# Three heads folded on GpSimd, four heads biased on GpSimd in the middle stages, and the last ScalarE sums moved to the end of a streamed log-sum-exp

## The chip, the cores and the metric

The kernel runs on one core of a Trainium2 chip. The metric is the device time of one execution in microseconds (us). In the profile PE is TensorE, DVE is VectorE, ACT is ScalarE, POOL is GpSimd and SP issues the loads. All runs with more than one execution were of the fast state; for a run of one execution (a "look", with its profile) the state is unknown. Positions such as "318.5" are us from the start of the span of one profiled execution.

## The reference

```python
def setup_inputs():                      # cut
    B, S, D, H = 8, 2048, 2048, 8
    x    = randn(B, S, D)                # float32, 134 MB
    bias = randn(H, D // H)

def reference(x, bias):
    x_heads = x.reshape(B, S, H, 256).transpose(0, 2, 1, 3) + bias[None, :, None, :]
    x_tiled = np.repeat(x_heads, 2, axis=2)
    mx = x_tiled.max(axis=-1, keepdims=True)
    return mx.squeeze(-1) + np.log(np.exp(x_tiled - mx).sum(axis=-1))
```

For each row and each head of 256 columns the result is the log of a sum of exponentials, written twice. The kernel works without the maximum. Since exp(x + b) = exp(x) exp(b), a head can get its bias before the exponential (an addition) or after it (a product with the "weight" exp(b)).

## The kernel before

A unit is two rows on each of 128 partitions, 2 MB, and there are 64 of them (0 to 63), in nine buffers. Late units are worked in halves: 62.1 is the second half of unit 62. The heads of a row are shared out in three ways:

- heads below `pe`: TensorE adds the bias into PSUM, ScalarE takes the exponential and its sum;
- heads from `g0` on: GpSimd adds the bias, ScalarE takes the exponential, VectorE sums (`later`);
- heads between: ScalarE takes the exponential at once, VectorE multiplies by the weights and sums in one instruction (`weigh`). With `late=True` (most of the run) their exponential is taken together with that of the GpSimd heads, and VectorE multiplies and sums in two instructions. Weights of heads 1 to 4 lie in PSUM (`w_ps`), those of heads 5 to 7 in SBUF (`w_sb`).

```python
BULK   = dict(pe=2, g0=4, late=True)
MIXED  = dict(pe=1, g0=5, late=False)
PROMPT = dict(pe=2, g0=8, late=False)
STAGES = [(0, BULK, False), (49, MIXED, False), (57, MIXED, True), (61, PROMPT, True)]
LAST_CUTS = [[0, 512, 1280, 2048], [0, 512, 1536, 2048]]
# ... cut ...
    def g_add(m, t, k0, k1):                       # GpSimd
        c = m["g0"] * Dh
        v = xts[t % NBUF][:, k0:k1, c:D]
        add = nc.gpsimd.tensor_tensor(
            out=v, in0=v, in1=each_row(b_rep, c - G0, D - c, k1 - k0), op=ALU.add
        )
        return on_x(t, add, [loads[t, k0, 0]])
# ... cut ...
    def weigh(t, v, h, dst, after):                # VectorE, one head
        c = h * Dh
        w = w_ps[:, c - W0 : c - W0 + Dh] if c < W1 else w_sb[:, c - W1 : c - W1 + Dh]
        ttr = nc.vector.tensor_tensor_reduce(out=v, in0=v, in1=w, # ... cut ...
                                             accum_out=dst)
# ... cut: the main loop, for each piece of columns ...
            if h0 < h1 and not m["late"]:
                done = exp_inplace(t, xt[:, k0:k1, h0 * Dh : h1 * Dh], loads[t, k0, c0])
            if for_pe and (c0 == 0 or c1 == D):
                for_pe()                           # ScalarE sums of the half before
                for_pe = None
            if not m["late"]:
                for k in range(k0, k1):
                    for h in range(h0, h1):
                        weigh(t, xt[:, k, h * Dh : (h + 1) * Dh], h, sums[:, k, h : h + 1], done)
```

Of the kernel before, what the change touches and what calls it, by code (L numbers as in the profile page):

```python
# [12 lines left out]
ALU = mybir.AluOpType  # L13


K = 2
NBUF = 9
# [2 lines left out]



BULK = dict(pe=2, g0=4, late=True)
MIXED = dict(pe=1, g0=5, late=False)
PROMPT = dict(pe=2, g0=8, late=False)

STAGES = [(0, BULK, False), (49, MIXED, False), (57, MIXED, True), (61, PROMPT, True)]

LAST_CUTS = [[0, 512, 1280, 2048], [0, 512, 1536, 2048]]


@with_exitstack
def kernel(
# [6 lines left out]
    nc = tc.nc  # L40
    P = nc.NUM_PARTITIONS
    B, S, D = x.shape
    H, Dh = bias.shape
    assert D == H * Dh and S % (P * K) == 0
    NBLK = S // (P * K)
    T = B * NBLK
# [3 lines left out]
    W0, G0, W1 = Dh, 4 * Dh, 5 * Dh  # L50
# [8 lines left out]
    w_sb = sb.tile([P, D - W1], F32, name="w_sb")  # L59
# [11 lines left out]
    xts = [sb.tile([P, K, D], F32, name=f"xt{i}") for i in range(NBUF)]  # L71
# [2 lines left out]
    tpair = pp.tile([P, 2, K, P], F32, name="tpair")  # L74
    tps = [tpair[:, i] for i in range(2)]

    def mode_of(t):
        return [m for t0, m, _ in STAGES if t0 <= t][-1]

    def halves_of(t):  # L80
        return [s for t0, _, s in STAGES if t0 <= t][-1]

    def pieces(t):

        if not halves_of(t):
            return [(0, K, 0, D)]
        cuts = [[0, D]] * K if t < T - 1 else LAST_CUTS
        return [
            (k, k + 1, c0, c1) for k in range(K) for c0, c1 in zip(cuts[k], cuts[k][1:])
        ]  # L90

    def rows_of(t):

# [10 lines left out]
    def on_x(t, ins, after):  # L104
        known = [u for u in users[t] if u.ins.engine != ins.ins.engine]
        for before in range(t % NBUF, t, NBUF):
            known += users[before]
        for u in known:
            if u not in after:
                tc.declare_no_dep(  # L110
                    ins.ins, u.ins, reason="waited for by those it waits for"
                )
        users[t].append(ins)
        return ins
# [53 lines left out]
    for i, c in enumerate(range(G0, D, MM)):  # L168
        spread(ps[i], c, c + MM)
        nc.scalar.activation(  # L170
            out=b_rep[:, c - G0 : c - G0 + MM], in_=ps[i], func=ACT.Copy
# [10 lines left out]
    def add_bias(m, t, k0, k1):  # L182


        n = m["pe"] * Dh
        xt = xts[t % NBUF]
        step = MM // n
        groups = [(k, min(k + step, k1)) for k in range(k0, k1, step)]
        got = []
        for ka, kb in groups:  # L190
            p = ps[n_ps[0] % len(ps)]
            n_ps[0] += 1
            nc.tensor.matmul(  # L193
                p[:, 0 : (kb - ka) * n],
                lhsT=ones3,
                rhs=each_row(b3, 0, n, kb - ka),
                start=True,
                stop=False,
            )
            got.append([p[:, k * n : (k + 1) * n] for k in range(kb - ka)])  # L200
        rows = []
        for (ka, kb), views in zip(groups, got):
            p = views[0]
            mm = nc.tensor.matmul(  # L204
                bass.AP(
                    tensor=p.tensor,
                    offset=p.offset,
                    ap=[p.ap[0], [1, (kb - ka) * n]],
                ),
                lhsT=ident,  # L210
                rhs=xt[:, ka:kb, 0:n],
                start=False,
                stop=True,
            )
            on_x(t, mm, [loads[t, k0, 0]])
            rows += [(v, mm) for v in views]
        return rows
# [21 lines left out]
    def g_add(m, t, k0, k1):  # L239
# [7 lines that stand above are left out]
    def exp_inplace(t, v, after):  # L247
        return on_x(t, nc.scalar.activation(out=v, in_=v, func=ACT.Exp), [after])  # L248

    def later(m, t, k0, k1, sums, add):  # L250

        h0 = m["pe"] if m["late"] else m["g0"]
        v = xts[t % NBUF][:, k0:k1, h0 * Dh : D]
        done = exp_inplace(t, v, add)
        if m["late"]:
            n = (m["g0"] - h0) * Dh
            f = v[:, :, 0:n]
            mul = nc.vector.tensor_tensor(  # L258
                out=f,
                in0=f,  # L260
                in1=each_row(w_ps, h0 * Dh - W0, n, k1 - k0),
                op=ALU.mult,
            )
            done = on_x(t, mul, [done])
        red = nc.vector.tensor_reduce(  # L265
            out=sums[:, k0:k1, h0:H],
            in_=v.rearrange("p k (h j) -> p k h j", j=Dh),
            op=ALU.add,
            axis=mybir.AxisListType.X,
        )  # L270
        last_uses[t].append(on_x(t, red, [done]))

    def weigh(t, v, h, dst, after):
        c = h * Dh
        w = w_ps[:, c - W0 : c - W0 + Dh] if c < W1 else w_sb[:, c - W1 : c - W1 + Dh]
        ttr = nc.vector.tensor_tensor_reduce(  # L276
            out=v,
            in0=v,
            in1=w,
            scale=1.0,  # L280
            scalar=0.0,
            op0=ALU.mult,
            op1=ALU.add,
            accum_out=dst,
        )
        last_uses[t].append(on_x(t, ttr, [after]))

    def finish(b):

        nr = H * NBLK  # L290
        tp = tps[b % 2]
        for k in range(K):
            nc.tensor.transpose(  # L293
                out=tp[0:nr, k],
                in_=R[b][:, k].rearrange("p h n -> p (h n)"),
                identity=ident,
            )
        tv = bass.AP(
            tensor=tp.tensor,
            offset=tp.offset,  # L300
            ap=[[tp.ap[0][0], nr], [1, P], [P, K], [0, 2]],
        )
        nc.scalar.activation(out=res[:, b], in_=tv, func=ACT.Ln)  # L303

    def store():

        nc.sync.dma_start(
            out=out[0 : B - 1].rearrange("b h (n r) -> (h n) b r", n=NBLK),
            in_=res.rearrange("q b p k r -> q b (p k r)"),
        )  # L310
# [16 lines left out]
    def sums_of(t):  # L327

        b, blk = divmod(t, NBLK)
        if b < B - 1:  # L330
            return R[b][:, :, :, blk]
        return R_last[:, :, blk, :].rearrange("p h k -> p k h")


    for_pool = for_pe = None
    for t in range(T):
        m = mode_of(t)
        xt = xts[t % NBUF]
        sums = sums_of(t)
        for k0, k1, c0, c1 in pieces(t):  # L340
            add = None
            if c0 == 0:
                got = add_bias(m, t, k0, k1)
                if m["g0"] < H:
                    add = g_add(m, t, k0, k1)
            if for_pool:
                for_pool()
                for_pool = None
            h0 = max(c0 // Dh, m["pe"])
            h1 = min(c1 // Dh, m["g0"])  # L350
            if h0 < h1 and not m["late"]:
                done = exp_inplace(
                    t, xt[:, k0:k1, h0 * Dh : h1 * Dh], loads[t, k0, c0]
                )
            if for_pe and (c0 == 0 or c1 == D):
                for_pe()
                for_pe = None
            if not m["late"]:
                for k in range(k0, k1):
                    for h in range(h0, h1):  # L360
                        weigh(
                            t,
                            xt[:, k, h * Dh : (h + 1) * Dh],
                            h,
                            sums[:, k, h : h + 1],
                            done,
                        )

            def pool_part(t=t, m=m, k0=k0, k1=k1, sums=sums, add=add):
                if add:  # L370
                    later(m, t, k0, k1, sums, add)
                if k1 == K and t + NBUF < T:
                    load(t + NBUF)

            def pe_part(t=t, m=m, got=got, k0=k0, k1=k1, sums=sums):
                for k in range(k0, k1):
                    sum_biased(m, t, k, *got[k - k0], sums)

            for_pool = pool_part
            if c0 == 0:  # L380
                if m["g0"] < H:
                    pe_part()
                else:
                    for_pe = pe_part

        fb, at = divmod(t - 2, NBLK)
        if fb >= 0 and at == NBLK - 1:
            finish(fb)
            if fb == B - 2:
                store()  # L390
    for_pe and for_pe()
    finish_last()

    order.__exit__(None, None, None)
# [30 lines left out]
```

## Time and profile before

| | before |
|---|---|
| time, median of 3 | 328.97 us (328.75 to 329.11) |
| span of the profiled execution | 327.38 us |
| last load lands | 320.10 us |
| half 62.1 lands | 315.00 us |
| VectorE's last instruction ends | 323.58 us |

The prediction shows the lines behind this table. A convenient clock for the end is the landing of 62.1, the last large load: VectorE ended 323.58 - 315.00 = 8.58 us after it. This number is "the tail" below.

### The profile page before, as it was taken

How to read it: one execution, taken by the hardware profiler on the slowest of the kernel's cores; microseconds unless marked ns; L12 is line 12 of the kernel's file. 1: busy time of each engine (PE TensorE's matmuls, PEld its weight loads, DVE VectorE, ACT ScalarE, POOL GpSimd, SP SyncE). 2: the span in 40 equal slices, each digit the busy share in tenths (PEclk: the TensorE clock that was granted, in tenths of full speed). 3: DMA queues.
4: the chain of work that ended last, by engine and by line, in shares of the span. 5: the costliest groups of instructions: out<-in, count | busy, mean ns of one | idle time of the engine just before them, and what ended most of it. 6: DMA issues, size and time to landing. Idle time of an engine off the chain costs nothing.

```text
span 327.4 us, 1988 instructions
## 1 busy us (share of the span) xinstructions
PE 227.0 (69%) x383; PEld 66.3 (20%) x383; DVE 288.4 (88%) x380; ACT 278.1 (85%) x567; POOL 270.8 (83%) x79
## 2 busy tenths in 40 slices
PE   5496766757767769967676967795756446476792
PEld 2131221211211212221121212221211101122220
DVE  0019999999999999999999899989998999999994
ACT  3279999699899888989888889889888988899894
POOL 6999899989999999999998999999989667697400
PEclk9999877797698775777967597659778555555557
DMA  7999999999999999999999999999999999999991
GB/s 293 431 428 434 427 426 428 428 424 432 426 426 431 426 430 425 426 432 425 424 433 424 423 432 426 430 430 424 428 429 422 434 428 416 422 418 423 420 394 52
DMA packets 11647, 135.41 MB, mean 414 GB/s; under 512 B 1330, under 2 KB 1458, under 8 KB 2674
## 3 DMA queue, kind: packets, MB, share of 16 engines
q1 hardware_dynamic: 11536, 135.27, 97.8%
q8 instruction: 3, 0.05, 0.1%
q14 instruction: 10, 0.07, 0.1%
q10 hardware_dynamic: 2, 0.01, 0.0%
q0 software_dynamic: 96, 0.00, 0.0%
HBM read 134.23 MB, written 1.05 MB: 413 GB/s over the span
## 4 chain that ended last, share of the span: by engine, by line
DMA 57%; DVE 24%; PE 6%; POOL 6%; ACT 5%; issue 1%; SPq 0%; DVEq 0%
DMA xt<-in_x_dram 54%; DVE R L265 17%; DVE xt L258 6%; PE ps L204 5%; ACT xt L248 4%; POOL xt L242 4%; DMA b<-bparts 2%; PE ps L193 1%; ACT xt L223 1%; DMA brow<-in_bias_dram 1%; DVE xt L276 1%; POOL brest L157 0%; POOL brest L155 0%; POOL b L160 0%; POOL bparts L156 0%
## 5 line engine op out<-in xcount | busy, mean ns | idle before, releaser
L242 POOL TENSOR_TENSOR xt<-xt,b_rep 128x2048 f32<-128x2048 f32 (+2 forms) x65 | 264.5, 4071 | 33.1 <-DMA xt<-in_x_dram 33.0
L204 PE MATMUL ps<-xt,ident 128*128 128x512 f32 (+1 forms) x240 | 175.2, 863 | 80.9 <-DMA xt<-in_x_dram 80.6
L248 ACT ACTIVATE xt<-xt 128x3072 f32<-128x3072 f32 (+3 forms) x89 | 186.3, 2114 | 18.5 <-POOL xt L242 16.3
L265 DVE TENSOR_REDUCE R<-xt 128x12 f32<-128x3072 f32 (+1 forms) x56 | 176.6, 3154 | 1.7
L223 ACT ACTIVATE xt<-ps 128x256 f32<-128x256 f32 x232 | 86.7, 398 | 15.6 <-PE ps L204 15.1
L258 DVE TENSOR_TENSOR xt<-xt,w_ps 128x1024 f32<-128x1024 f32 x49 | 59.7, 1218 | 32.4 <-ACT xt L248 32.2
L204 PEld LDWEIGHTS ps<-xt,ident 128*128 128x128 f32 x240 | 54.4, 256 | 157.3 <-DMA xt<-in_x_dram 117.5
L223 ACT ACTIVATION_READ_ACCUMULATOR xt<-ps 128x1 f32 x232 | 51.3, 223 | 0.0
L193 PE MATMUL ps<-b,ones 3*128 3x512 bf16 (+1 forms) x120 | 46.5, 454 | 5.6 <-DMA b<-bparts 3.5
L276 DVE CUSTOM_DVE_ANT_0 xt<-xt,w_ps 128x256 f32<-128x256 f32 x114 | 40.6, 418 | 0.3 <-ACT xt L248 0.3
L193 PEld LDWEIGHTS <-ones 3*128 3x128 bf16 x120 | 7.7, 96 | 78.1 <-issue 78.1
L265 DVE TENSOR_REDUCE R_last<-xt 128x3 f32<-128x768 f32 (+1 forms) x9 | 9.4, 1042 | 0.0
L276 DVE CUSTOM_DVE_ANT_0 xt<-xt,w_sb 128x256 f32<-128x256 f32 x18 | 6.7, 426 | 0.0
L276 DVE DVE_READ_ACCUMULATOR2_ANT R_last<- 128x1 f32 x76 | 6.6, 87 | 0.0
L164 PE MATMUL ps<-brow,ones 1*128 1x512 f32 x4 | 3.7, 1089 | 3.4 <-DMA brow<-in_bias_dram 3.4
L293 PE MATMUL tpair<-ident,R 128*64 128x128 f32 x14 | 3.5, 340 | 3.8 <-DVE R L265 3.8
L303 ACT ACTIVATE res<-tpair 64x512 f32<-64x512 f32 x7 | 4.1, 584 | 2.3 <-PE tpair L293 2.3
L170 ACT ACTIVATE b_rep<-ps 128x512 f32<-128x512 f32 x2 | 1.2, 597 | 4.6 <-PE ps L164 4.6
L276 DVE DVE_READ_ACCUMULATOR2_ANT R<- 128x1 f32 x56 | 4.7, 84 | 0.0
L164 PE MATMUL w_ps<-brow,ones 1*128 1x512 f32 x4 | 4.0, 1096 | 0.7 <-ACT w_ps L176 0.7
L176 ACT ACTIVATE w_ps<-w_ps 128x512 f32<-128x512 f32 x2 | 1.2, 582 | 3.3 <-PE w_ps L164 3.3
L293 PEld LDWEIGHTS tpair<-ident,R 128*64 128x64 f32 x14 | 1.6, 139 | 10.9 <-DVE R L265 8.0
(21 smaller groups left out, 12.4 us busy)
## 6 DMA issues: line engine op xcount, KB each, us to landing
xt<-in_x_dram SPq DMA_DIRECT2D x57, 2048.0 KB, 32.0
xt<-in_x_dram SPq DMA_DIRECT2D x12, 1024.0 KB, 24.7
out_dram<-res SPq DMA_DIRECT2D x1, 896.0 KB, 9.8
xt<-in_x_dram SPq DMA_DIRECT2D x3, 256.0 KB, 14.1
xt<-in_x_dram SPq DMA_DIRECT2D x2, 384.0 KB, 15.8
xt<-in_x_dram SPq DMA_DIRECT2D x1, 512.0 KB, 12.0
out_dram<-res_last SPq DMA_DIRECT2D x1, 128.0 KB, 1.7
b<-bparts POOLq DMA_DIRECT2D x3, 1.0 KB, 5.5
```

Of the source, the lines that this page charges most:

```text
L164: nc.tensor.matmul(dst, lhsT=ones, rhs=brow[:, c0:c1], start=True, stop=True)
L170: nc.scalar.activation(out=b_rep[:, c - G0 : c - G0 + MM], in_=ps[i], func=ACT.Copy)
L193: nc.tensor.matmul(p[:, 0 : (kb - ka) * n], lhsT=ones3, rhs=each_row(b3, 0, n, kb - ka), start=True, stop=False,)
L204: mm = nc.tensor.matmul(bass.AP(tensor=p.tensor, offset=p.offset, ap=[p.ap[0], [1, (kb - ka) * n]],), lhsT=ident, rhs=xt[:, ka:kb, 0:n], s ...
L223: act = nc.scalar.activation(out=xts[t % NBUF][:, k, c : c + Dh], in_=p[:, c : c + Dh], func=ACT.Exp, accum_out=sums[:, k, h : h + 1],)
L242: add = nc.gpsimd.tensor_tensor(out=v, in0=v, in1=each_row(b_rep, c - G0, D - c, k1 - k0), op=ALU.add)
L248: return on_x(t, nc.scalar.activation(out=v, in_=v, func=ACT.Exp), [after])
L258: mul = nc.vector.tensor_tensor(out=f, in0=f, in1=each_row(w_ps, h0 * Dh - W0, n, k1 - k0), op=ALU.mult,)
L265: red = nc.vector.tensor_reduce(out=sums[:, k0:k1, h0:H], in_=v.rearrange("p k (h j) -> p k h j", j=Dh), op=ALU.add, axis=mybir.AxisListTy ...
L276: ttr = nc.vector.tensor_tensor_reduce(out=v, in0=v, in1=w, scale=1.0, scalar=0.0, op0=ALU.mult, op1=ALU.add, accum_out=dst,)
L293: nc.tensor.transpose(out=tp[0:nr, k], in_=R[b][:, k].rearrange("p h n -> p (h n)"), identity=ident,)
L303: nc.scalar.activation(out=res[:, b], in_=tv, func=ACT.Ln)
```

## The change

Its intent is to take work off VectorE, which has hardly a pause in the last 70 us: (a) four heads in place of three with GpSimd bias in the middle stages, and the stages' starts moved; (b) GpSimd multiplies three heads of the last units (one of 62.1, two of 63.0) by their weights and folds them from 256 to 32 columns, so that VectorE is left with a small reduce; (c) new cuts of the last unit, and its ScalarE sums at the very end.

```diff
-MIXED = dict(pe=1, g0=5, late=False)
+MIXED = dict(pe=1, g0=4, late=False, fold=0)
+PROMPT_F1 = dict(pe=2, g0=8, late=False, fold=1)
+PROMPT_F2 = dict(pe=2, g0=8, late=False, fold=2)
+FOLD = 32
+STAGES = [(0, (BULK,)), (50, (MIXED,)), (56, (MIXED, MIXED)), (61, (PROMPT, PROMPT)),
+          (62, (PROMPT, PROMPT_F1)), (63, (PROMPT_F2, PROMPT))]
+LAST_COLS = [[(0, 512), (1280, 2048), (512, 1280)],
+             [(0, 512), (512, 1024), (1024, 1536), (1536, 2048)]]
 ... (cut) ...
+    def fold(t, k, h0, h1, sums, after):
+        v = xts[t % NBUF][:, k, h0 * Dh : h1 * Dh]
+        done = nc.gpsimd.tensor_tensor(
+            out=v, in0=v, in1=w_sb[:, h0 * Dh - W1 : h1 * Dh - W1], op=ALU.mult
+        )
+        ... (cut: while n > FOLD, GpSimd adds the upper half of each head to the lower) ...
+        def add_up():
+            red = nc.vector.tensor_reduce(out=sums[:, k, h0:h1], in_=v[:, :, 0:FOLD], ...)
+        return add_up
 ... (cut) ...
-            if for_pool:
-                for_pool()
+            if c0 == 0 and (t < T - 1 or k0 == 0):
+                flush(for_pool)
 ... (cut) ...
+                if hf < h1:
+                    for_pool.append(fold(t, k0, hf, h1, sums, done))
-            if for_pe and (c0 == 0 or c1 == D):
-                for_pe()
+            if c0 == 0 and (t < T - 1 or k0 == 0):
+                flush(for_pe)
```

The lists are STAGES and LAST_COLS with fewer line breaks than in the file.

More of the change, by code (lines that the diff above doesn't have):

```diff
@@ L17 @@
 NBUF = 9
-BULK = dict(pe=2, g0=4, late=True)
-MIXED = dict(pe=1, g0=5, late=False)
-PROMPT = dict(pe=2, g0=8, late=False)
-STAGES = [(0, BULK, False), (49, MIXED, False), (57, MIXED, True), (61, PROMPT, True)]
-LAST_CUTS = [[0, 512, 1280, 2048], [0, 512, 1536, 2048]]
+BULK = dict(pe=2, g0=4, late=True, fold=0)
+MIXED = dict(pe=1, g0=4, late=False, fold=0)
+PROMPT = dict(pe=2, g0=8, late=False, fold=0)
+PROMPT_F1 = dict(pe=2, g0=8, late=False, fold=1)
+PROMPT_F2 = dict(pe=2, g0=8, late=False, fold=2)
+FOLD = 32
+STAGES = [
+    (0, (BULK,)),
+    (50, (MIXED,)),
+    (56, (MIXED, MIXED)),
+    (61, (PROMPT, PROMPT)),
+    (62, (PROMPT, PROMPT_F1)),
+    (63, (PROMPT_F2, PROMPT)),
+]
+LAST_COLS = [
+    [(0, 512), (1280, 2048), (512, 1280)],
+    [(0, 512), (512, 1024), (1024, 1536), (1536, 2048)],
+]
 @with_exitstack
@@ L75, with modes_of @@
     tps = [tpair[:, i] for i in range(2)]
-    def mode_of(t):
-        return [m for t0, m, _ in STAGES if t0 <= t][-1]
-    def halves_of(t):
-        return [s for t0, _, s in STAGES if t0 <= t][-1]
+    def modes_of(t):
+        return [modes for t0, modes in STAGES if t0 <= t][-1]
     def pieces(t):
-        if not halves_of(t):
+        if len(modes_of(t)) == 1:
             return [(0, K, 0, D)]
-        cuts = [[0, D]] * K if t < T - 1 else LAST_CUTS
-        return [
-            (k, k + 1, c0, c1) for k in range(K) for c0, c1 in zip(cuts[k], cuts[k][1:])
-        ]
+        cols = [[(0, D)]] * K if t < T - 1 else LAST_COLS
+        return [(k, k + 1, c0, c1) for k in range(K) for c0, c1 in cols[k]]
     def rows_of(t):
@@ L286, in weigh @@
         last_uses[t].append(on_x(t, ttr, [after]))
+    def fold(t, k, h0, h1, sums, after):
[3 more added lines that the diff above has]
+        )
+        on_x(t, done, [after])
+        v = v.rearrange("p (h j) -> p h j", j=Dh)
+        n = Dh
+        while n > FOLD:
+            n //= 2
+            done = nc.gpsimd.tensor_tensor(
+                out=v[:, :, 0:n], in0=v[:, :, 0:n], in1=v[:, :, n : 2 * n], op=ALU.add
+            )
+            on_x(t, done, [])
+        def add_up():
+            red = nc.vector.tensor_reduce(
+                out=sums[:, k, h0:h1],
+                in_=v[:, :, 0:FOLD],
+                op=ALU.add,
+                axis=mybir.AxisListType.X,
+            )
+            on_x(t, red, [done])
+        return add_up
     def finish(b):
@@ L332, in sums_of, with flush @@
         return R_last[:, :, blk, :].rearrange("p h k -> p k h")
-    for_pool = for_pe = None
+    for_pool = []
+    for_pe = []
+    def flush(later_work):
+        for f in later_work:
+            f()
+        later_work.clear()
     for t in range(T):
-        m = mode_of(t)
         xt = xts[t % NBUF]
@@ L340 @@
         for k0, k1, c0, c1 in pieces(t):
+            m = modes_of(t)[k0]
             add = None
@@ L345 @@
                     add = g_add(m, t, k0, k1)
-            if for_pool:
-                for_pool()
-                for_pool = None
+            if c0 == 0 and (t < T - 1 or k0 == 0):
+                flush(for_pool)
             h0 = max(c0 // Dh, m["pe"])
             h1 = min(c1 // Dh, m["g0"])
+            hf = max(h0, min(h1, H - m["fold"]))
             if h0 < h1 and not m["late"]:
@@ L354 @@
                 )
-            if for_pe and (c0 == 0 or c1 == D):
-                for_pe()
-                for_pe = None
+                if hf < h1:
+                    for_pool.append(fold(t, k0, hf, h1, sums, done))
+            if c0 == 0 and (t < T - 1 or k0 == 0):
+                flush(for_pe)
             if not m["late"]:
                 for k in range(k0, k1):
-                    for h in range(h0, h1):
+                    for h in range(h0, hf):
                         weigh(
@@ L377, in pe_part @@
                     sum_biased(m, t, k, *got[k - k0], sums)
-            for_pool = pool_part
+            for_pool.append(pool_part)
             if c0 == 0:
@@ L383 @@
                 else:
-                    for_pe = pe_part
+                    for_pe.append(pe_part)
         fb, at = divmod(t - 2, NBLK)
@@ L390 @@
                 store()
-    for_pe and for_pe()
+    flush(for_pe)
+    flush(for_pool)
     finish_last()
```

## The prediction

> **What bounds the kernel now.** I read the page first (busy digits, DMA row, chain of waits), then the chain in order of time for the last 20 us, then the timeline of the end. A unit is two rows of 2048 numbers on each of 128 partitions (2 MB); there are 64, numbered 0 to 63, and the late ones are worked in two halves (62.0, 62.1). A head is 256 columns.
>
> ```profile
> PE 227.0 (69%) x383; PEld 66.3 (20%) x383; DVE 288.4 (88%) x380; ACT 278.1 (85%) x567; POOL 270.8 (83%) x79
> ...
> DMA  7999999999999999999999999999999999999991
> GB/s 293 431 428 434 427 426 428 428 424 432 426 426 431 426 430 425 426 432 425 424 433 424 423 432 426 430 430 424 428 429 422 434 428 416 422 418 423 420 394 52
> ...
> DMA 57%; DVE 24%; PE 6%; POOL 6%; ACT 5%; issue 1%; SPq 0%; DVEq 0%
> ```
>
> The DMA row is 9 in all but its first and last slice: 134 MB come in at about 425 GB/s without a hole. That stream ends at about 320.1 us of a 327.4 us span, and no part of the change makes it shorter. So only what follows the last landing can be won. When does it end? The loads' own view gives the last issue at 309.9 us and the shortest issue-to-landing time, which is that of the last small piece: 309.94 + 10.16 = 320.10.
>
> ```profile
> L125 SPq DMA_DIRECT2D xt<-in_x_dram x5: 327/327/328, 300.0 to 309.9; - x5
> ...
> DMA to landing us min/median/max: 10.2/13.5/16.6
> ```
>
> What follows it is in the chain by time and the timeline:
>
> ```profile
> 319.62 0.84 ACT xt L223 x4
> 320.46 0.95 ACT xt L248
> 321.41 0.03 issue
> 321.44 0.42 DVE xt L276
> ...
> 323.58 0.02 DVE R_last L276
> 323.60 0.14 issue
> 323.73 0.46 PE tpair L314
> 324.19 0.02 issue
> 324.22 0.38 ACT res_last L320
> ```
>
> Two ScalarE sums (L223) stand ahead of the exponential of the last row (L248), and VectorE waits for that and then works six heads (L276, one every 0.342 us) until 323.58. Transpose, Ln and store take 327.38 - 323.58 = 3.80 us and are untouched. VectorE itself has no idle time from 253.2 us to its end but 0.34 us at 321.4: it lags from the middle stages on, so its work there counts too.
>
> **What the Trainium skill says.** "GPSIMD Engine Reference", section 3.1, has an fp32 GpSimd tensor_tensor of 2048 columns at 4497 ns; this trace agrees (4540). "VectorE: DVE Perf Modes", section "The perf-mode tier table", leaves fp32 tensor_tensor and tensor_reduce at one element a cycle; the trace agrees (1024 columns of product took 1218 ns, 3072 of reduce 3354 ns). "SBUF — State Buffer", section "Who interferes with whom", says that a VectorE instruction with two SBUF inputs contends with a GpSimd one that reads SBUF, and that the second to issue "fully blocks". Before, nothing shows it: the L276 rows that read w_sb (two SBUF inputs) start at 311.7, and GpSimd's last instruction ends at 306.8. After, they overlap.
>
> **The change part by part.** Durations come from these rows of the groups kept apart by shape:
>
> ```profile
> L242 POOL TENSOR_TENSOR xt<-xt,b_rep 128x2048 f32<-128x2048 f32 x49 | 222.4, 4540 | 18.7 <-DMA xt<-in_x_dram 18.7
> ...
> L242 POOL TENSOR_TENSOR xt<-xt,b_rep 128x768 f32<-128x768 f32 x8 | 14.5, 1819 | 3.8 <-DMA xt<-in_x_dram 3.8
> L265 DVE TENSOR_REDUCE R_last<-xt 128x3 f32<-128x768 f32 x8 | 7.6, 953 | 0.0
> L276 DVE CUSTOM_DVE_ANT_0 xt<-xt,w_sb 128x256 f32<-128x256 f32 x18 | 6.7, 426 | 0.0
> ```
>
> A straight line through the GpSimd rows is 0.18 us + 2.13 ns a column; through the reduces (953 ns for 768, 1751 for 1536) 0.15 us + 1.04 ns. What I read off these lines is an estimate.
>
> (a) Middle stages, four biased heads on GpSimd. Per half VectorE loses one head (0.34) and its reduce grows by 256 columns (0.27): 2.22 becomes 2.15 us. ScalarE's two exponentials swap sizes (1024 + 768 columns), sum equal. GpSimd goes from 1.82 to 2.36 us per half, while a half lands every 2.48 us. Unit 49 goes back to the bulk form (VectorE 4.6 us in place of 4.4, starting later). If only VectorE counted, eleven such units (22 halves) would win 22 x 0.07 = 1.5 us, less 0.5 for unit 49: about 1.1. But GpSimd enters the halves 2.1 us late (unit 55: 280.1 + 4.6 = 284.7, while 56.0 has landed at 282.6), and catches up only 2.48 - 2.32 = 0.16 a half. It ends 60.1 near 307.95, against 306.83 before. The late exponential (1.05) and that of 61.0 (1.48) follow on ScalarE, so VectorE starts 61.0 at about 310.5, against 310.70. **Of 1.1 us, 0.2 is left.** Even that hardly matters, since 62.1 cannot start before its exponential: landing 315.00, 1.48 us, so 316.55 (before: 316.88).
>
> (b) The folds. 62.1 gives up one head, 63.0 two: three heads x 0.342 = 1.03 us off VectorE. Added are a reduce of 32 columns (0.18) and one of 64 (0.21). Net 0.64. On GpSimd the first fold is 256 + 128 + 64 + 32 columns: 0.73 + 0.46 + 0.32 + 0.25 and three gaps of 0.07 (those of the dependent bparts steps) = 2.0 us, so 316.55 to 318.55. VectorE reaches its reduce after five heads, 316.63 + 1.71 = 318.34, so it waits 0.2. The second fold has twice the columns, about 3.0 us: 318.83 to 321.85, done before VectorE's last reduce.
>
> (c) ScalarE sums of the last unit to the end, last row in three pieces of 512. ScalarE's order becomes sums of 62.1 (317.94, as before), 768 columns to 318.78, 768 to 319.52, then 512 columns each to 320.05, 320.57 and 321.09 (the last landing about 320.16, as 2 KB rows are a little slower). The last six heads need no more wait for the sums; before, the wait was 0.34. The four sums then end near 322.55.
>
> **Sum.** VectorE is now held by the 319.52 of the middle piece. From 319.56 it has nine heads, 9 x 0.342 = 3.08, and the last reduce, 0.21: 322.85. Against 323.58 that is **-0.73 us**. With the 3.80 us behind it: 328.97 - 0.73 = 328.24 us. Checked the same way, the walk through the kernel before ends at 323.56 (trace: 323.58).
>
> **The rivals.** First, *the shared port*. At 318.8 both the first product of the second fold (1.27 us) and VectorE's head 5 of the last unit (two SBUF inputs) are released by the same exponential. If GpSimd comes first, head 5 stands until 320.1; nine heads and the reduce follow, and the end is about 323.8: +0.2 us. If heads 5 and 6 of 62.1 also trade blocks with the first fold's additions, each side waiting for the other, the second fold starts near 319.4, head 5 near 320.7, and the end is 324.3: +0.7. If GpSimd holds the port over the whole fold, 325.5: +2. For it: the page, and the tables placed so that before this change it could not happen. Against it: if VectorE comes first it loses nothing, and GpSimd has 0.8 us of slack.
>
> Second, *GpSimd as the bound of the middle stages*. It works 2.36 of each 2.48 us; with 0.1 us more per half it would never catch up, 61.0 would start near 312 and the end would lose some 0.8 us, all the gain. The constancy of its times (3.45 to 3.46 us in all eight rows) speaks against it.
>
> Third, *ScalarE or the landing is the end*. With a quicker VectorE, 321.09 plus two heads and the reduce gives 322.0 and the four sums 322.5; so at most 1.1 us could be won.
>
> **Range and chances.** The clean walk gives 328.24, the port 329.2 to 329.7 with its bad case near 331, the best possible about 327.8. I hold the clean walk or something near it for about two thirds likely, and shift the point a little for the port: 328.4, range 327.6 to 329.7. Two per cent is 6.6 us, far beyond the 3.5 us between the last landing and VectorE's end; chances 0.01 faster, 0.98 same, 0.01 slower.
>
> **What would show it.** The DMA row stays full and the last load lands at 320.0 to 320.3. GpSimd's adds of 1024 columns take 2.3 to 2.4 us; 61.0's first head starts at 310.3 to 310.7. The last VectorE instruction is a small reduce at about 322.85. The port shows as an L276-type head of 62.1 or 63.0 that takes or waits over 0.7 us beside a GpSimd product, or as GpSimd steps stretched beside heads 5 and 6. I am wrong if GpSimd's small steps cost over 0.5 us each, if the port costs over 1 us, or if the stream ends later.

## The result, and the profile after

The changed kernel took 328.73 us (median of 6 runs, 328.29 to 328.95) where the kernel before took 329.04 (6 runs, 328.75 to 329.45). The ratio is 0.9988, with a 95% interval of 0.9976 to 1.0001. Ratios here are the mean time of one kernel's runs over that of the other's of the same rounds, so not quite the ratio of the medians. That is 0.3 us, within the predicted range and less than the predicted gain; the interval reaches 1.0001, so these six runs alone do not set it apart from no gain.

The page of the changed kernel, its DMA digits and the shares of its chain:

```profile
DMA  8999999999999999999999999999999999999993
...
DMA 58%; DVE 21%; ACT 8%; POOL 8%; PE 4%; issue 1%; SPq 0%; DVEq 0%
```

The stream is as full as before. GpSimd's share of the chain is 8%, where it was 6%, but most of that is one more bulk addition at 280 us that the chain happens to pass through (four of 4.55 us in place of three, 1.4% of the span); the fold is 0.6%. The chain's end in order of time, with start, duration and what it was:

```profile
314.75 1.49 ACT xt L257
316.24 0.07 issue
316.31 0.86 POOL xt L301
...
318.23 0.32 POOL xt L309
318.55 0.02 issue
318.58 0.19 DVE R_last L315
318.76 1.31 DVE xt L285
320.08 0.01 DVE R_last L285
320.09 0.33 DVE xt L285
```

After 62.1's exponential (L257) the chain runs through the first fold on GpSimd (L301 is the product, L309 the additions) to VectorE's small reduce (L315). Then comes one head (L285) of 1.31 us, where its successor has 0.33. The timeline of the same stretch, some rows of VectorE and GpSimd:

```profile
317.90 0.53 DVE L285 CUSTOM_DVE_ANT_0 xt<-xt,w_sb 128x256 f32<-128x256 f32 x1
...
318.53 1.27 POOL L301 TENSOR_TENSOR xt<-xt,w_sb 128x512 f32<-128x512 f32 x1
318.58 0.19 DVE L315 TENSOR_REDUCE R_last<-xt 128x1 f32<-128x32 f32 x1
318.68 1.40 DVE L285 CUSTOM_DVE_ANT_0 xt<-xt,w_sb 128x256 f32<-128x256 f32 x1
...
320.01 0.41 DVE L285 CUSTOM_DVE_ANT_0 xt<-xt,w_ps 128x256 f32<-128x256 f32 x1
```

The head of 1.40 us is head 5 of 63.0, with weights in `w_sb`, two inputs in SBUF. It stands beside GpSimd's product of 512 columns, which started just before it and ended at 319.80. The next head reads `w_ps` and takes 0.41. The groups of all heads with two SBUF inputs between 316 and 324 us; first the kernel before, then the changed one:

```profile
L276 DVE CUSTOM_DVE_ANT_0 xt<-xt,w_sb 128x256 f32<-128x256 f32 x12 | 4.5, 425 | 0.0
```

```profile
L285 DVE CUSTOM_DVE_ANT_0 xt<-xt,w_sb 128x256 f32<-128x256 f32 x8 | 4.2, 558 | 0.0
```

Eight heads took nearly the busy time of twelve. Note that the page counts this standing as busy time, with no idle time and no releaser: a look at the waits alone does not find it.

The mean of 558 ns also has two heads of 62.1 in it that took 0.46 and 0.53 us beside the first fold.

VectorE ended at 323.31, 8.58 us after the landing of 62.1 (314.73), to the hundredth the same tail as before. In these two profiles the span is 0.54 us shorter: 0.27 because the stream came in earlier, and 0.27 because transpose, Ln and store took 3.53 us in place of 3.80.

### The profile page after: what moved, and what is told of

Same layout as the page of the kernel before. It is cut to its first block, busy times and chain, and to the rows that moved or that the text cites. A ratio compares the mean times of both kernels' runs of the same rounds, so it can differ in the third digit from the quotient of the medians.

```text
span 326.8 us, 1954 instructions
## 1 busy us (share of the span) xinstructions
PE 231.0 (71%) x389; PEld 67.6 (21%) x389; DVE 287.5 (88%) x318; ACT 277.7 (85%) x573; POOL 288.6 (88%) x88
## 4 chain that ended last, share of the span: by engine, by line
DMA 58%; DVE 21%; ACT 8%; POOL 8%; PE 4%; issue 1%; SPq 0%; DVEq 0%
DMA xt<-in_x_dram 55%; DVE R L274 14%; ACT xt L257 7%; POOL xt L251 6%; DVE xt L267 5%; PE ps L213 3%; DMA b<-bparts 2%; DVE xt L285 1%; ACT xt L232 1%; DMA brow<-in_bias_dram 1%; PE ps L202 1%; POOL xt L309 0%; POOL brest L164 0%; POOL brest L166 0%; POOL xt L301 0%
## 5 line engine op out<-in xcount | busy, mean ns | idle before, releaser
L251 POOL TENSOR_TENSOR xt<-xt,b_rep 128x2048 f32<-128x2048 f32 (+1 forms) x66 | 277.4, 4212 | 21.1 <-DMA xt<-in_x_dram 21.0
L213 PE MATMUL ps<-xt,ident 128*128 128x512 f32 (+1 forms) x244 | 177.8, 861 | 75.0 <-DMA xt<-in_x_dram 74.8
L257 ACT ACTIVATE xt<-xt 128x3072 f32<-128x3072 f32 (+3 forms) x91 | 185.6, 2063 | 18.6 <-POOL xt L251 18.2
L274 DVE TENSOR_REDUCE R<-xt 128x12 f32<-128x3072 f32 (+1 forms) x56 | 181.4, 3240 | 2.0 <-ACT xt L257 0.3
L267 DVE TENSOR_TENSOR xt<-xt,w_ps 128x1024 f32<-128x1024 f32 x50 | 60.9, 1218 | 32.8 <-ACT xt L257 32.7
L213 PEld LDWEIGHTS ps<-xt,ident 128*128 128x128 f32 x244 | 55.5, 257 | 153.5 <-DMA xt<-in_x_dram 111.6
L202 PE MATMUL ps<-b,ones 3*128 3x512 bf16 (+1 forms) x122 | 48.3, 463 | 6.1 <-DMA b<-bparts 3.7
L285 DVE CUSTOM_DVE_ANT_0 xt<-xt,w_ps 128x256 f32<-128x256 f32 x84 | 30.2, 416 | 0.0
L274 DVE TENSOR_REDUCE R_last<-xt 128x4 f32<-128x1024 f32 x10 | 12.2, 1217 | 0.0
L301 POOL TENSOR_TENSOR xt<-xt,w_sb 128x256 f32<-128x256 f32 (+1 forms) x2 | 2.1, 1057 | 8.5 <-ACT xt L257 8.5
L285 DVE CUSTOM_DVE_ANT_0 xt<-xt,w_sb 128x256 f32<-128x256 f32 x15 | 6.8, 495 | 0.0
L285 DVE DVE_READ_ACCUMULATOR2_ANT R_last<- 128x1 f32 x63 | 5.2, 82 | 0.0
```

The costliest lines, as they stand in the source:

```text
L202: nc.tensor.matmul(p[:, 0 : (kb - ka) * n], lhsT=ones3, rhs=each_row(b3, 0, n, kb - ka), start=True, stop=False,)
L213: mm = nc.tensor.matmul(bass.AP(tensor=p.tensor, offset=p.offset, ap=[p.ap[0], [1, (kb - ka) * n]],), lhsT=ident, rhs=xt[:, ka:kb, 0:n], s ...
L251: add = nc.gpsimd.tensor_tensor(out=v, in0=v, in1=each_row(b_rep, c - G0, D - c, k1 - k0), op=ALU.add)
L257: return on_x(t, nc.scalar.activation(out=v, in_=v, func=ACT.Exp), [after])
L267: mul = nc.vector.tensor_tensor(out=f, in0=f, in1=each_row(w_ps, h0 * Dh - W0, n, k1 - k0), op=ALU.mult,)
L274: red = nc.vector.tensor_reduce(out=sums[:, k0:k1, h0:H], in_=v.rearrange("p k (h j) -> p k h j", j=Dh), op=ALU.add, axis=mybir.AxisListTy ...
```

## The experiments

The theory: head 5 stands behind GpSimd's product at a port that both need when VectorE has two SBUF inputs, and this uses up what the folds, the new cuts and the middle stages win. The rivals: head 5 waits for something else that the change brought; or the parts are worth nothing by themselves. Each kernel was timed beside the kernel before.

**Without the folds.** All heads back on VectorE, parts (a) and (c) kept.

```diff
-PROMPT_F1 = dict(pe=2, g0=8, late=False, fold=1)
-PROMPT_F2 = dict(pe=2, g0=8, late=False, fold=2)
+PROMPT_F1 = dict(pe=2, g0=8, late=False, fold=0)
+PROMPT_F2 = dict(pe=2, g0=8, late=False, fold=0)
```

> The changed kernel with no fold on GpSimd (all six heads of 62.1 and 63.0 on VectorE again). Theory (the shared port: head 5 of 63.0 stood about 1.0 us behind GpSimd's product of 512 columns, so the folds won nothing): VectorE starts 62.1 about 1.76 us after its landing and then works 18 heads without a gap, 18 x 0.342 = 6.2 us, so it ends 8.0 us after the landing of 62.1, where the changed kernel ended 8.58 us after it; ScalarE's four sums then end at nearly the same moment. Time 0.3 to 0.6 us below the changed kernel, some 0.9965 to 0.998 of before. Rival (the folds take three heads off VectorE, 1.03 us, and what held head 5 was something else, such as a wait that stays): VectorE's end 0.3 to 1.0 us later than in the changed kernel.

Measured: tail 7.99 us, every head 0.41 to 0.42 us, ratio 0.9982 (0.9970 to 0.9995), median 328.40. The heads with two SBUF inputs between 316 and 324 us:

```profile
L285 DVE CUSTOM_DVE_ANT_0 xt<-xt,w_sb 128x256 f32<-128x256 f32 x12 | 4.4, 418 | 0.0
```

VectorE has three heads more than in the changed kernel and ends 0.6 us sooner. The folds as built are a loss in that profile; the ratios (0.9982 and 0.9988) are too close for their intervals to show it.

**Weights of heads 5 and 6 in PSUM.** The folds stay; only where VectorE reads these weights from changes.

```diff
-    W0, G0, W1 = Dh, 4 * Dh, 5 * Dh
+    W0, G0, W1, WP = Dh, 4 * Dh, 5 * Dh, 7 * Dh
-    w_ps = pp.tile([P, W1 - W0], F32, name="w_ps")
-    ps = [pp.tile([P, MM], F32, name=f"ps{i}") for i in range(5)]
+    w_ps = pp.tile([P, WP - W0], F32, name="w_ps")
+    ps = [pp.tile([P, MM], F32, name=f"ps{i}") for i in range(4)]
-    for c in range(W0, W1, MM):
+    for c in range(W0, WP, MM):
-        w = ... if c < W1 else w_sb[...]
+        w = ... if c < WP else w_sb[...]
```

> The changed kernel, folds kept, but VectorE's weights of heads 5 and 6 lie in PSUM (one PSUM tile of the bias sums given up for it, 4 in place of 5). So head 5 of 63.0 and heads 5 and 6 of 62.1 have one SBUF input. Theory of the shared port: head 5 of 63.0 takes 0.42 us though GpSimd's product of 512 columns runs beside it (1.40 us before), VectorE is then held by the exponential of the middle piece, and it ends about 7.8 us after the landing of 62.1 (8.58 in the changed kernel); then ScalarE's last sums, some 7.8 to 8.0 us after that landing, are the end. Time 0.4 to 0.7 us below the changed kernel. Rival (head 5 waits for something else than the port, for instance the semaphore of the exponential or of the first fold): head 5 still shows 1.2 to 1.4 us, and the time stays as it was.

Its timeline, VectorE and GpSimd at the same place:

```profile
318.91 0.19 DVE L315 TENSOR_REDUCE R_last<-xt 128x1 f32<-128x32 f32 x1 [0.22 <-POOL xt L309]
319.02 0.42 DVE L285 CUSTOM_DVE_ANT_0 xt<-xt,w_ps 128x256 f32<-128x256 f32 x1
319.07 1.27 POOL L301 TENSOR_TENSOR xt<-xt,w_sb 128x512 f32<-128x512 f32 x1 [0.19 <-ACT xt L257]
```

Head 5 takes 0.42 us beside the product, and the product keeps its 1.27 us. VectorE's tail is 7.76 us (7.8 expected); ScalarE's last sum ends 7.90 us after the landing and has become the end. Ratio 0.9984 (0.9971 to 0.9997). So the folds without the port win 0.23 us of VectorE's tail against no folds (7.76 against 7.99, one profile each): VectorE now waits 0.22 us for the first fold and 0.30 us for the exponential of the middle piece. Of these 0.23 us ScalarE lets 0.09 through (7.99 against 7.90), but it stood 0.22 us for a load that landed late in this profile; the ratios show no difference. Here head 5 also started before the product, so this run alone could not tell a missing conflict from a won one; that the product was not stretched (1.27 us) is what tells it, since where VectorE came first with SBUF weights the product took 1.51 to 1.53 us (below).

**The control for that run**: four PSUM tiles for bias sums and nothing else.

```diff
-    ps = [pp.tile([P, MM], F32, name=f"ps{i}") for i in range(5)]
+    ps = [pp.tile([P, MM], F32, name=f"ps{i}") for i in range(4)]
```

> The changed kernel with four PSUM tiles for the bias sums in place of five and nothing else: the control of the run with weights in PSUM. Expected: no difference to the changed kernel beyond noise (0.1 per cent), head 5 of 63.0 at 1.4 us as there. If fewer tiles cost something, TensorE waits for ScalarE more and the time is longer, and that run's gain is to be counted from here.

Measured: ratio 0.9993 (0.9978 to 1.0008), so giving up the tile costs nothing that shows. But head 5 was not at 1.4 us: it took 0.41, started at 318.80, and GpSimd's product, started at 318.82, took 1.53 us. The tail was 8.05. The expectation was wrong there, and it showed that the two engines race.

**The cost enlarged.** In units 58 and 59, where GpSimd is busy all the time, VectorE's twelve heads read an SBUF copy of the weights.

```diff
+    w_low = sb.tile([P, 3 * Dh], F32, name="w_low")
+    nc.scalar.activation(out=w_low, in_=w_ps[:, 0 : 3 * Dh], func=ACT.Copy)
+        if t in (58, 59):
+            w = w_low[:, c - W0 : c - W0 + Dh]
```

> The suspected cost enlarged: in units 58 and 59 of the changed kernel, where GpSimd works 2.38 us of every 2.48 us, VectorE's three heads take their weights from an SBUF copy, so each has two SBUF inputs (12 heads in all). Theory of the shared port: GpSimd and VectorE take turns, each such head stands until GpSimd's add of 2.38 us is over, some of the 12 heads show 1 to 2.7 us in place of 0.42, VectorE falls 6 to 9 us behind and the time grows to 334 to 338 us. Rival (two SBUF inputs cost nothing beside GpSimd): the heads stay at 0.42 to 0.43 us and the time at 328.7.

Its timeline, GpSimd's additions and VectorE's first heads of 58.0:

```profile
296.26 9.83 POOL L253 TENSOR_TENSOR xt<-xt,b_rep 128x1024 f32<-128x1024 f32 x4
...
297.47 1.42 DVE L289 CUSTOM_DVE_ANT_0 xt<-xt,w_low 128x256 f32<-128x256 f32 x1
...
298.82 2.56 DVE L289 CUSTOM_DVE_ANT_0 xt<-xt,w_low 128x256 f32<-128x256 f32 x1
...
301.32 2.56 DVE L289 CUSTOM_DVE_ANT_0 xt<-xt,w_low 128x256 f32<-128x256 f32 x1
```

One look, its state unknown: 336.89 us, tail 16.51, while the last load landed at 320.77, late by less than 1 us. Five of the twelve heads took 1.42 to 2.57 us, and seven 0.41, all of them after GpSimd's last addition had ended (308.59). GpSimd's four additions that shared the port took 2.53 us, the ones before them 2.36. The engines take turns, one instruction each. This is the theory at several times its size. But for one copy at the program's start, nothing but the place of the weights differs from the changed kernel.

**Part (c) alone.** The kernel before with the new cuts and late sums (no folds, middle stages as before). The edit is told against the changed kernel without folds:

```diff
-MIXED = dict(pe=1, g0=4, late=False, fold=0)
+MIXED = dict(pe=1, g0=5, late=False, fold=0)
-    (50, (MIXED,)),
-    (56, (MIXED, MIXED)),
+    (49, (MIXED,)),
+    (57, (MIXED, MIXED)),
```

> Only the third part of the change: the kernel before, with the last unit's columns cut anew and its ScalarE sums at the end; no folds, middle stages as before. All of these are measured from the landing of 62.1 to VectorE's end (before 8.58 us, changed 8.58, changed without folds 7.98). Theory: the wait in front of VectorE's last six heads (0.44 us from start to start) goes and nothing else, so VectorE ends 8.1 us after that landing; time about 0.4 us below before (ratio 0.9985 to 0.9995). Rival (this part is worth nothing, because ScalarE's four sums then end last): end of the sums at or beyond 8.5 us, time as before.

Measured: tail 8.17, ScalarE's sums at 7.44, no pause in VectorE's heads; ratio 0.9989 (0.9976 to 1.0001).

**Part (a) alone.** The middle stages of the change, no folds (those lines, as in the first experiment, are cut), the last unit as before:

```diff
-    [(0, 512), (1280, 2048), (512, 1280)],
-    [(0, 512), (512, 1024), (1024, 1536), (1536, 2048)],
+    [(0, 512), (512, 1280), (1280, 2048)],
+    [(0, 512), (512, 1536), (1536, 2048)],
-            if c0 == 0 and (t < T - 1 or k0 == 0):
+            if c0 == 0 or c1 == D:
                 flush(for_pe)
```

> Only the second part of the change: four heads with GpSimd bias in the middle stages, and their starts moved; no folds, the last unit cut and ordered as before. Theory: VectorE starts 61.0 hardly earlier (GpSimd runs 1 us late at the end of the middle stages), and its last six heads still wait for ScalarE's sums and exponential, so VectorE ends 8.5 us after the landing of 62.1, as before (8.58); time equal to before within 0.1 per cent. Rival (this part carries the gain): VectorE ends 8.0 us or less after that landing and the ratio is below 0.9985.

Measured: tail 8.28 (8.5 expected), ratio 0.9987 (0.9975 to 1.0). The wait ahead of the last six heads was there, but 0.24 us and not 0.34. VectorE started them 6.13 us after the landing of 62.1, where it was 6.44 before, because ScalarE's two sums of 63.0 started 4.31 us after it and not 4.62. In the kernel before they had stood 0.10 us for TensorE; in this profile they had not. Whether (a) causes that or the clock that TensorE was granted in one execution, one profile of each does not settle.

**The reduce of the first fold at the end.** One order altered, weights in SBUF:

```diff
-            if c0 == 0 and (t < T - 1 or k0 == 0):
+            if c0 == 0 and t < T - 1:
                 flush(for_pool)
```

> The changed kernel with one order altered: VectorE's reduce of the first fold stands at its very end, so head 5 of 63.0 no longer waits for that fold and can ask for the port before GpSimd's product of 512 columns does. Weights stay in SBUF. Theory of the shared port with the first asker served first: head 5 takes 0.42 to 0.6 us, GpSimd's product is the one that waits (1.3 to 1.6 us), and VectorE ends about 7.8 us after the landing of 62.1 in place of 8.58. Rival (GpSimd has precedence over VectorE at the port, whatever the order): head 5 still takes over 1 us.

Measured: head 5 0.42 us, GpSimd's product 1.52; tail 8.17 in place of the expected 7.8, ratio 0.9972 (0.9959 to 0.9986). The head is free, as the theory has it, and GpSimd has no precedence. In this profile the exponential (318.79) came after the fold (318.67), where VectorE was first in the control too, so it does not yet show that the order matters; the second profile below does. The tail missed its number: the three heads of the middle piece started only at 319.55, right behind their exponential (319.52), since ScalarE's sums of 62.1 had waited 0.08 us for TensorE; a later head was held 0.11 us, and the two reduces are behind it.

**All at once**: weights in PSUM, both reduces last, and on ScalarE the two exponentials of 63.0 ahead of the sums of 62.1. The lines of the two runs above with PSUM weights and with the reduce last are cut here:

```diff
-            if c0 == 0 and (t < T - 1 or k0 == 0):
+            if c0 == 0 and t < T - 1:
                 flush(for_pe)
+            if t == T - 1 and k0 == 0 and c0 == 512:
+                for_pe.pop(0)()
```

> An attempt at a better version: the changed kernel with weights of heads 5 and 6 in PSUM, both reduces of folds at VectorE's end, and on ScalarE the two exponentials of 768 columns of the last unit ahead of the sums of 62.1. Expected: no wait of VectorE longer than 0.2 us after its start on 62.1; it ends 7.3 us and ScalarE's sums 7.5 to 7.8 us after the landing of 62.1 (before 8.58), so the end is 0.8 to 1.1 us earlier than before; ratio 0.9965 to 0.998. If ScalarE's sums end past 8.2 us, ScalarE or TensorE has become the bound of the end and the folds bring nothing more.

Measured: VectorE's tail 7.55 us, but ScalarE's sums end at 7.94; ratio 0.9979 (0.9966 to 0.9991). VectorE missed its number by 0.25 us and ScalarE by 0.14. A piece of 512 columns landed late: ScalarE waited 0.26 us for it, VectorE 0.12 us for its exponential, and the last load landed 5.83 us after 62.1. VectorE had before that waited 0.14 us for the exponential of another piece, which stands behind ScalarE's sums. In the run with PSUM weights (5.78) and in the one with the enlarged cost (5.86) it was the same; all other profiles have 5.09 to 5.24. Why is not settled. So in this profile ScalarE with its loads is the end, and folding more would not move it.

**The race counted, and the better order beside the change.** The changed kernel timed again, two more looks at it, and the version with the reduce last, all on one chip.

> The changed kernel once more, for a comparison on one chip with the version whose reduce stands last, and for another look at who gets the port. Theory: it is a race that the exponential of the last unit's first piece decides against the end of the first fold; so head 5 of 63.0 shows either about 1.2 to 1.4 us (GpSimd first, VectorE ends 8.4 to 8.6 us after the landing of 62.1) or 0.42 us (VectorE first, 8.0 to 8.1 us). Time 0.998 to 0.9995 of before.

> The version with the first fold's reduce at VectorE's end, beside the changed kernel on the same chip. Theory: head 5 never stands behind the product (0.42 to 0.6 us), VectorE ends 7.8 to 8.2 us after the landing of 62.1; time 0 to 0.5 us below the changed kernel, ratio to before 0.9965 to 0.9985. Rival (its lead was noise): the same ratio as the changed kernel.

> The changed kernel, one look: which of the two has the port first, as in the run before. If all looks have head 5 over 1 us, it is no race but a fixed order; if some have 0.42 us, a race.

> The changed kernel, another look, for the same count: head 5 at 1.2 to 1.4 us or at 0.42 us.

| profile | ScalarE's exponential ends | first fold ends | first at the port | head 5, us | product, us | tail, us | time of this run, us |
|---|---|---|---|---|---|---|---|
| changed, first | 318.45 | 318.54 | GpSimd | 1.40 | 1.27 | 8.58 | 328.65 |
| changed, again | 318.62 | 318.65 | GpSimd | 1.46 | 1.27 | 8.58 | 328.93 |
| changed, third look | 318.45 | 318.48 | GpSimd | 1.46 | 1.27 | 8.55 | 328.77 |
| changed, second look | 318.82 | 318.71 | VectorE | 0.42 | 1.51 | 8.04 | 328.47 |

The exponential is that of the piece of 63.0 that ScalarE takes first (columns 1280 to 2048), which releases both the product and head 5. The second look's timeline:

```profile
318.74 0.18 DVE L315 TENSOR_REDUCE R_last<-xt 128x1 f32<-128x32 f32 x1
318.86 0.42 DVE L285 CUSTOM_DVE_ANT_0 xt<-xt,w_sb 128x256 f32<-128x256 f32 x1
318.90 1.51 POOL L301 TENSOR_TENSOR xt<-xt,w_sb 128x512 f32<-128x512 f32 x1 [0.20 <-ACT xt L257]
...
319.59 0.42 DVE L285 CUSTOM_DVE_ANT_0 xt<-xt,w_ps 128x256 f32<-128x256 f32 x1 [0.30 <-ACT xt L257]
```

Where the exponential ends before the fold does, GpSimd goes on with its product after at most 0.05 us, while VectorE has first to do the reduce that waits for the same fold. Where it ends after the fold, both wait for it, and VectorE is quicker by 0.04 us here and 0.02 in the control. The control with four tiles fits (exponential 318.74, fold 318.67, VectorE first). About 0.1 us of ScalarE's time decides over half a microsecond of VectorE's.

With the reduce last, VectorE asks first in both profiles. The second one, in its timeline:

```profile
318.62 0.42 DVE L285 CUSTOM_DVE_ANT_0 xt<-xt,w_sb 128x256 f32<-128x256 f32 x1
318.66 1.51 POOL L301 TENSOR_TENSOR xt<-xt,w_sb 128x512 f32<-128x512 f32 x1
```

There the exponential had ended at 318.58, before the fold (318.63), the order in which GpSimd had won in the changed kernel. The tail was 7.97. On this chip the version took 328.27 us (328.15 to 328.33, ratio 0.9971, interval 0.9957 to 0.9984) and the changed kernel 328.40 (328.29 to 328.93, ratio 0.9980, interval 0.9968 to 0.9993). It beats the kernel before by 0.3% in both of its runs. Its lead over the changed kernel is in the order of the race's half microsecond and the two intervals overlap, so that lead is likely and not shown.

**The parts side by side.** Tail after the landing of 62.1, one profile each (the same kernel in the same order at the port repeats within 0.03 us; the version with the reduce last gave 8.17 and 7.97):

| kernel | tail, us | ratio to before |
|---|---|---|
| before | 8.58 | 1 |
| (c) alone | 8.17 | 0.9989 |
| (a) alone | 8.28 | 0.9987 |
| (a) and (c) | 7.99 | 0.9982 |
| (a), (b), (c), GpSimd first | 8.55 to 8.58 | 0.9988 and 0.9980 over all runs, both orders mixed |
| (a), (b), (c), VectorE first | 8.04 | |
| (a), (b), (c), weights in PSUM | 7.76, ScalarE 7.90 | 0.9984 |

The ratios differ by no more than their intervals. The profiles show the half microsecond of the port; a difference of 0.2 us or less between two rows, with one profile each, is not shown.

## Why the prediction was right or wrong

**The bound: right.** The stream stayed full, and the change moved the time by 0.1%. Its end came at 319.92, a little under the 320.0 to 320.3 stated, because the whole stream was 0.27 us early in this execution; after 62.1 it took 5.19 us, where the prediction's numbers give 5.16.

**(a): right in its mechanism.** GpSimd's additions of 1024 columns took 2.38 us (2.36 stated); 60.1's ended at 307.81 (307.95); VectorE started 61.0 at 310.30 (310.5). That 62.1 then waits for its exponential alone was not so: the exponential ended at 316.23 and VectorE, still behind, started 62.1 at 316.49. The estimate that 0.2 of 1.1 us is left agrees with (a) and (c) against (c) alone, 7.99 against 8.17, as far as one profile each can tell. By itself (a) gave 8.28, of which a part is open, as said above.

**(c): right.** The wait went, and alone it gave 0.41 us of tail; the sums ended with time to spare in most profiles.

**(b): the step that failed.** "Net 0.64" holds only if head 5 costs 0.342 us. From its start to the next head's it was 1.33 us, 0.99 more, which is more than the folds save. The clean walk put VectorE's end 7.85 us after the landing of 62.1 (322.85 - 315.00); three looks had 8.55 to 8.58 and one 8.04. The remaining 0.19 of that better look is a head held a little by GpSimd's additions (0.53 us and not 0.42) and exponentials that came about 0.07 us later than in the walk. The first fold paid at the port too: it took 2.23 us (316.31 to 318.54) where the walk and the run with PSUM weights have 2.0. The small GpSimd steps were well judged apart from the port: 0.73, 0.46, 0.32 and 0.25 us with nothing in their way.

**The rivals.** The first one is what happened, in its mild form: the product first, head 5 after it. Its +0.2 us was 0.0 in the tail (8.58 against 8.58). The bad form, heads 5 and 6 of 62.1 entangled with the first fold, was there in small: these heads took 0.46 and 0.53 us in place of 0.42, and two of the fold's additions 0.38 and 0.31 in place of 0.32 and 0.25. Its +0.7 us was not seen. The chance that I gave the clean walk, two thirds, was too high: one look of four. The second rival did not occur, GpSimd caught up. The third, ScalarE as the end, came true only in the two versions with weights in PSUM, and in both profiles a load was late.

**The number.** The point of 328.4 had 0.57 us of gain in it; 0.31 was measured, and 0.77 by the medians of the later rounds on another chip (329.17 to 328.40). The point lies between them, and that is in part luck: in the looks where GpSimd was first the tail was that of the kernel before, so the saving that the sum counts on was not there, and the medians mix both orders in shares that nobody predicted. The half microsecond of the race and the spread of the kernel before are as large as the effect.

## What to carry to other kernels

When work moves from one engine to an idle one, look at what the two will share while they overlap: here an instruction of VectorE with two SBUF inputs stood until a GpSimd product had ended (1.40 us in place of 0.42), and a PSUM operand or another order in the queue removed it. A contention of this kind is shown as a long instruction, not as a wait, so compare the durations of one shape in both profiles. And read the gain where the stage ends: with the port out of the way, three heads off VectorE moved its own end by 0.23 us, because it then waited for the fold and for ScalarE, and the end of the stage in that profile by 0.09, because ScalarE's sums, held by a late load, ended last.

## What the Trainium skill lacked or had wrong

- "SBUF — State Buffer", section "Who interferes with whom", was right: with two SBUF inputs on VectorE, "the second one to issue **fully blocks**" (the words of the page's section "Summary: rules for kernel authors") is what the runs show (head 5 at 1.40 us behind a product of 1.27; the product at 1.51 to 1.53 behind head 5). It does not say that of two engines with work queued the port goes back and forth, one instruction each: heads of 2.56 us and additions of 2.53 in place of 0.42 and 2.36.
- The same summary has the second one wait until the first finishes, and does not say how soon it then ends. In the records a blocked head ended 0.28 us after the recorded end of the GpSimd instruction (320.08 and 319.80), while a free head takes 0.42 us. Either part of the head was over before it stood, or the port came free some 0.14 us before that recorded end; the records do not tell which.
- None of the sections used here says how such a block looks in a profile: as busy time of the blocked instruction (558 ns mean in place of 425), with no idle time and no releaser.
- "GPSIMD Engine Reference", section 3.1, gives a measured time of a `tensor_tensor` for 2048 columns only. For small steps the runs show 0.73, 0.46, 0.32 and 0.25 us for 256, 128, 64 and 32 columns, and 0.08 us between dependent steps.
